# One token group of a mixer interleaved with the MLP before it, with the on-chip memory laid out from two sides

## The chip, the cores and the metric

The kernel runs on one core of one Trainium2 chip. The core has five engines that work side by side, each down its own list of instructions: PE (matrix multiplication), DVE (vector), ACT (scalar and activation functions), POOL (a second, general elementwise engine) and SP, which here only issues DMA transfers. They meet through semaphores. Data lies in device memory (HBM), in SBUF (the on-chip memory that all engines read) and in PSUM (eight banks of accumulators that PE writes). The metric is the device time of one execution in microseconds (us); lower is better. Before the change three runs took 2917.79, 2919.15 and 2923.32 us, median 2919.15 us.

## What is computed

One inference step of a two-layer hybrid decoder of width 1024, on 16 meta tokens and 1024 prompt tokens of one sequence and 8 decode tokens of other sequences, 1048 tokens in all, in float32. Cut to what matters:

```python
def _trunk(h, ...):
    for i in range(2):
        hn = _rmsnorm(h, norm_mix[i])
        if i == 0: out = _conformer_conv(hn, ...)   # gated projection, 31-tap causal conv, LayerNorm, SiLU, projection
        else:      out = _rwkv7(hn, ...)            # r, k, v projections, low-rank decay/gate, sequential state update
        h = h + out
        h = h + _sqrelu_mlp(_rmsnorm(h, norm_mlp[i]), w_mlp_in[i], w_mlp_out[i])
    return _rmsnorm(h, norm_final)

def _sqrelu_mlp(h, w_in, w_out):                    # 1024 -> 4096 -> 1024
    return jnp.square(jax.nn.relu(h @ w_in)) @ w_out

def _rwkv7(h, ...):
    prev = h shifted by one token;  xx = prev - h
    xr, xw, xk, xv, xa, xg = (h + xx * x_mix[j] for j in range(6))
    r, k, v = xr @ w_r, xk @ w_k, xv @ w_v
    decay, a, g = low-rank functions of xw, xa, xg
    ... a state update per token, a group norm, (yn + bonus) * g @ w_o
```

The new states (convolution rows, shifted row, the RWKV matrices) are outputs too.

## The kernel before

**Precision.** Every float32 product is three passes of PE (`mm3`, L185): weight and activation are each split into a high part (a cast on ACT, L157) and a low part, the difference (L162, on POOL in four pieces of 256 columns, or on DVE in one instruction of 1024), and PE computes high x high, low x high and high x low (L187 to L189).

**Weights.** `load_w` brings a 128 x 1024 block (512 KB) by a DMA on SP's list into a "raw" buffer (L146), and splits it into a "hi" and a "lo" buffer. A raw buffer comes free after the low part is made, hi and lo after the last matmul that reads them. The first layer has five raw and five split buffers for all its weights, the mixer three and four (`open_weights`), the rest five and five.

**Tokens.** The first layer works on three groups of 352, 348 and 348 tokens (`G0`), the mixer on four of 272, 256, 256 and 264 (`G1`), the end on three (`G2`). Between the layers the residual goes to HBM (`d_h`) and its normed form too (`d_hn`), and the mixer loads its own groups from `d_hn`.

**First layer.** For each group: `pw1` and the convolution (on DVE, in PSUM), `ln_silu`, then `post(g)`: the projection `pw2`, `mlp_in` (the norm's statistics and the split of the activations) and `mlp`. The MLP has 32 input blocks (`load_in`, `inp`, L327 to L329 and L141 behind the matmuls) and 32 output halves (`load_out`, `out`, L340), each block with 24 matmuls. Beside the MLP of one group run, as generators that `fill` advances at given points, the norm of the group before (`norm_out(g - 1)`, L591 to L605) and the convolution of the next. `norm_out(2)` stands behind the last MLP.

**Mixer.** Everything of the first layer is then closed (`with ExitStack() as l0`), its memory and PSUM handed to the mixer's pools: masks, `wk` (state of the recurrence), `tmp1`, `hnp`, weights, `mixp` (ten mixes), and the PSUM pools `psum1`, `psx1`, `psw`. `prepare(g)` loads the normed tokens and subtracts neighbours (L791). `mixer_in(g, tick, ahead)` makes eight mixes (L814, split by L140 and L141), eight r projections (copied by L965, stored to `d_rk` by L966), then the same for k with the gate's second layer, then for v with all that the recurrence needs (L1083 to L1126), stored to HBM. Beside the r projections runs the narrow first layer of the gate, beside the k projections that of decay and rate. Between the parts of each projection stands a call of `tick`, 72 in a group, which for groups 1 to 3 advances the recurrence over chunks of 64 tokens (`advance`) by a set pace; for group 0 the pace is 0, since no chunk is ready. In the front of each chunk L1214 masks a PSUM result into `nr`, once for each half.

**What sets the order.** The program is written in one order, with generators woven in by hand, and the tile framework's scheduler (`schedule_with_timeline_sim=True`) then places the instructions of every engine by that priority and its own estimate of times, subject to free buffers. On the chip each engine follows its list.

Of the kernel before, what the change touches and what calls it, by code (L numbers as in the profile page):

```python
# [16 lines left out]
P = 128  # L17
# [31 lines left out]
def hybrid_step(tc, x_prompt, x_sample, state_conv, state_shift, state_wkv, meta_tokens,  # L49
# [10 lines left out]
    with ctx:  # L60
# [63 lines left out]
        def open_tmp(stack, nmax, tag, bufs=3, **kw):  # L124
            cur["n"] = cur["wide"] = nmax
            cur["tmp"] = pool(stack, f"tmp{tag}", bufs, **kw)
            cur["stat"] = pool(stack, f"stat{tag}", 1, **kw)

        def stat(name, tag, bufs, w=None):
            return cur["stat"].tile([P, w or cur["n"]], F32, name=name, tag=tag, bufs=bufs)  # L130

        def open_weights(stack, raw_bufs, bufs, tag):
            if raw_bufs:
                cur["raw"] = pool(stack, f"wraw{tag}", raw_bufs)
            cur["wsp"] = pool(stack, f"wsp{tag}", 1)
            cur["bufs"] = bufs
# [12 lines left out]
        def load_w(src, shape, name, eng_lo, tag="w", raw=None):  # L149
# [4 lines left out]
            nb = cur["bufs"][tag]  # L154
            hi = cur["wsp"].tile([P, 8 * P], F32R, name=f"{name}_hi", tag=tag + "h", bufs=nb)
            lo = cur["wsp"].tile([P, 8 * P], F32R, name=f"{name}_lo", tag=tag + "l", bufs=nb)
# [16 lines left out]
        def col_stream(cols, raw_ahead, split_ahead, tag="w"):  # L173

            raws, parts = {}, {}
            for i in range(len(cols)):
                for j in range(i, min(i + raw_ahead + 1, len(cols))):
                    if j not in raws:
                        raws[j] = load_raw(col_src(*cols[j][:2]), (KT, P), cols[j][2])
                for j in range(i, min(i + split_ahead + 1, len(cols))):  # L180
                    if j not in parts:
                        parts[j] = load_w(None, (KT, P), cols[j][2], cols[j][3], tag, raws[j])
                yield parts[i]
# [7 lines left out]
        def bank(name, tag="mm"):  # L191
            return cur[tag].tile([P, 512], F32, name=name, tag=tag)

        def dense(w, act, n, name, fill=None):
            ps = bank(f"ps_{name}")
            for k in range(KT):
                mm3(ps[:, :n], (w[0][:, k, :], w[1][:, k, :]), (act[0][:, k, :n], act[1][:, k, :n]), k == 0, k == KT - 1)
                if fill and k == KT // 2 - 1:
                    fill()
            return ps  # L200
# [84 lines left out]
        def filler(points, *streams):  # L285
# [10 lines left out]
            return fill, chain.from_iterable(it for it, _ in its)  # L296
        MLP_POINTS = 6 * DFF // P
# [5 lines left out]
        def mlp(layer, groups, lag, eng_w, eng_h, fill=None, done=None):  # L303

# [14 lines left out]
            def inp(j, w, group):  # L319
# [4 lines left out]
                ps = dense(w, (ah, al), n, f"in{layer}_{j}_{gn}", fill)  # L324
# [7 lines left out]
            def out(b, i, w, group):  # L332
                gn, hv, n, ah, al, rs, hid_pool = group
                hh, hl = hid[gn, b]
                for m in range(4):
# [5 lines left out]
                    if fill:  # L341
                        fill()
# [1277 lines left out]
```

## Time and profile before

| | |
|---|---|
| median of three runs | 2919.15 us |
| the profiled execution, its span | 2917.4 us |
| mean granted clock of PE | 0.954 |
| DVE / ACT / POOL busy | 1974.6 / 1348.5 / 1698.8 us |
| DMA moved | 428.34 MB, mean 147 GB/s |
| projection pw2 of the last group | 822 to 863 us |
| MLP of the last group | 863 to 1122 us |
| from there to the first r projection of mixer group 0 | 1122 to 1149 us |
| mixer group 0, to the first r projection of group 1 | 1149 to 1302 us |

How to read it. The profile is one execution on the chip; the program's span there is 2917.4 us, and no other time is given for that execution. The page gives busy time by engine and the chain of work that ended last. A row of the view by stretches has start and end, length, the busy time of PE, of PE's weight loads, of DVE, ACT and POOL (with instruction counts), the granted clock of PE (1.00 is full), the busy share of the DMA engines and GB/s. In a timeline a row is start, duration, engine, line and operation, and in square brackets how long the engine had been idle and what ended that. A view of waits has who waited for whom: total us, times, longest. A group row has the operation, its tiles and shapes, the count, the busy time and the mean in ns, and the idle time before. Matmuls overlap, so their durations are longer than their distance from one another.

### The profile page before, as it was taken

The page shows a single profiled execution, that of the slowest core. Times are in us where ns is not written, and L with a number is a line of the kernel's source. Part 1 is how long each engine was busy: PE and PEld are TensorE (multiplying, and loading weights), DVE is VectorE, ACT ScalarE, POOL GpSimd, SP SyncE. Part 2 cuts the span into 40 slices and gives each one's busy share as a digit, 9 for nine tenths or more (in the row PEclk, how much of TensorE's full clock was granted, in tenths as well). Part 3 has the DMA queues.
Part 4 walks back from the last instruction along what each step waited for, and adds up shares of the span by engine and source line. Part 5 has one row for each costly group of instructions (what it writes and reads, how often), then busy time and mean ns, then how long its engine had stood idle before and what let it go on. Part 6 is the DMA issues. An engine that isn't in the chain of part 4 may idle for free.

```text
span 2917.4 us, 54478 instructions
## 1 busy us (share of the span) xinstructions
PE 2716.8 (93%) x20554; PEld 2578.6 (88%) x20554; DVE 1974.6 (68%) x3794; ACT 1348.5 (46%) x2515; POOL 1698.8 (58%) x2295
## 2 busy tenths in 40 slices
PE   8999999999999896879798899799999999999998
PEld 7988999999999896868688788677879999999998
DVE  5999999994554545477986885565697664444444
ACT  5546444543453333554667756443434453222223
POOL 6677778887797774443434454443447883333332
PEclk9999999999999998979899999889999999999999
DMA  6663444454444542667788867844557652222211
GB/s 176 172 183 95 149 139 134 140 173 138 138 139 142 173 130 89 203 190 193 195 201 228 229 189 185 228 108 124 139 134 218 184 158 84 70 68 68 71 59 40
DMA packets 659285, 428.34 MB, mean 147 GB/s; under 512 B 126840, under 2 KB 609208, under 8 KB 659022
## 3 DMA queue, kind: packets, MB, share of 16 engines
q1 hardware_dynamic: 652780, 421.93, 51.0%
q10 hardware_dynamic: 6018, 2.89, 0.4%
q8 instruction: 162, 2.65, 0.4%
q14 instruction: 101, 0.83, 0.1%
q0 software_dynamic: 224, 0.03, 0.0%
HBM read 353.03 MB, written 72.66 MB: 146 GB/s over the span
## 4 chain that ended last, share of the span: by engine, by line
PE 66%; DVE 13%; POOL 6%; DMA 5%; issue 4%; ACT 3%; SPq 0%; DVEq 0%; POOLq 0%; ACTq 0%
PE ps_in L189 7%; PE ps_in L187 7%; PE ps_in L188 7%; PE out L187 7%; PE out L189 7%; PE out L188 7%; POOL wo_lo L162 4%; POOL wi_lo L162 2%; DVE cv L504 2%; PE A L1206 2%; PE ps_o L189 1%; PE ps_o L188 1%; PE ps_o L187 1%; DVE mx L814 1%; PE ps_oo L187 1%
## 5 line engine op out<-in xcount | busy, mean ns | idle before, releaser
L162 POOL TENSOR_TENSOR wo_lo<-wo_raw,wo_hi 128x256 fp32r<-128x256 f32 x736 | 562.2, 796 | 300.0 <-ACT wo_hi L157 281.4
L162 POOL TENSOR_TENSOR wi_lo<-wi_raw,wi_hi 128x256 fp32r<-128x256 f32 x640 | 486.5, 792 | 308.2 <-ACT wi_hi L157 292.3
L187 PE MATMUL out<-hh,wo_hi 128*128 128x352 f32 (+2 forms) x1536 | 503.5, 328 | 21.0 <-DVE h L340 10.4
L340 DVE TENSOR_TENSOR h<-h,out 128x352 f32<-128x352 f32 (+2 forms) x768 | 385.3, 510 | 199.3 <-PE out L189 198.8
L189 PE MATMUL out<-hl,wo_hi 128*128 128x352 f32 (+2 forms) x1536 | 494.5, 324 | 7.0 <-DVE hl L141 7.0
L187 PE MATMUL ps_in<-m_h,wi_hi 128*128 128x352 f32 (+2 forms) x1536 | 498.4, 325 | 0.7 <-DVE h L340 0.7
L189 PE MATMUL ps_in<-m_l,wi_hi 128*128 128x352 f32 (+2 forms) x1536 | 498.2, 325 | 0.0
L188 PE MATMUL out<-hh,wo_lo 128*128 128x352 f32 (+2 forms) x1536 | 497.7, 324 | 0.0
L188 PE MATMUL ps_in<-m_h,wi_lo 128*128 128x352 f32 (+2 forms) x1536 | 497.0, 324 | 0.0
L504 DVE SCALAR_TENSOR_TENSOR cv<-u,wdw,cv 128x352 f32<-128x352 f32 (+2 forms) x720 | 376.9, 573 | 0.7
L157 ACT CAST wi_hi<-wi_raw 128x1024 fp32r<-128x1024 f32 x160 | 167.7, 1048 | 401.6 <-PE out L189 205.3
L157 ACT CAST wo_hi<-wo_raw 128x1024 fp32r<-128x1024 f32 x184 | 192.9, 1049 | 302.8 <-PE out L189 144.8
L187 PEld LDWEIGHTS out<-hh,wo_hi 128*128 128x128 f32 x1536 | 291.8, 190 | 28.1 <-DVE h L340 14.0
L189 PEld LDWEIGHTS out<-hl,wo_hi 128*128 128x128 f32 x1536 | 291.2, 190 | 9.4 <-DVE hl L141 8.3
L187 PEld LDWEIGHTS ps_in<-m_h,wi_hi 128*128 128x128 f32 x1536 | 291.2, 190 | 3.0 <-issue 0.9
L188 PEld LDWEIGHTS out<-hh,wo_lo 128*128 128x128 f32 x1536 | 291.8, 190 | 1.4
L189 PEld LDWEIGHTS ps_in<-m_l,wi_hi 128*128 128x128 f32 x1536 | 291.0, 190 | 2.0
L188 PEld LDWEIGHTS ps_in<-m_h,wi_lo 128*128 128x128 f32 x1536 | 290.9, 189 | 1.7
L327 DVE SCALAR_TENSOR_TENSOR r<-ps_in,rs_m 128x352 f32<-128x352 f32 (+2 forms) x192 | 98.6, 515 | 228.2 <-PE ps_in L189 224.5
L141 DVE TENSOR_TENSOR hl<-s,hh 128x352 fp32r<-128x352 f32 (+2 forms) x192 | 150.2, 783 | 102.4 <-ACT hh L140 102.3
L329 ACT ACTIVATE s<-r 128x352 f32<-128x352 f32 (+2 forms) x192 | 93.8, 490 | 146.8 <-DVE r L327 146.4
L162 POOL TENSOR_TENSOR wv_lo<-wv_raw,wv_hi 128x256 fp32r<-128x256 f32 x96 | 80.3, 866 | 28.9 <-ACT wv_hi L157 28.8
(407 smaller groups left out, 6248.1 us busy)
## 6 DMA issues: line engine op xcount, KB each, us to landing
wi_raw<-in_w_mlp_in_dram SPq DMA_DIRECT2D x160, 512.0 KB
wo_raw<-in_w_mlp_out_dram SPq DMA_DIRECT2D x160, 512.0 KB
wr_raw<-in_rwkv_w_r_dram SPq DMA_DIRECT2D x32, 512.0 KB
wk_raw<-in_rwkv_w_k_dram SPq DMA_DIRECT2D x32, 512.0 KB
wv_raw<-in_rwkv_w_v_dram SPq DMA_DIRECT2D x32, 512.0 KB
d_ab<-ab SPq DMA_DIRECT2D x32, 512.0 KB
pg_raw<-in_conv_w_pw_dram SPq DMA_DIRECT2D x24, 512.0 KB
pa_raw<-in_conv_w_pw_dram SPq DMA_DIRECT2D x24, 512.0 KB
```

The lines of the kernel that those rows point to most:

```text
L141: eng_lo.tensor_sub(lo, src, hi.bitcast(F32))
L157: nc.scalar.copy(hi[:, :a * b], raw[:, :a * b])
L162: eng_lo.tensor_sub(lo[:, cs], raw[:, cs], hi[:, cs].bitcast(F32))
L187: nc.tensor.matmul(ps, w[0], act[0], start=first, stop=False)
L188: nc.tensor.matmul(ps, w[1], act[0], start=False, stop=False)
L189: nc.tensor.matmul(ps, w[0], act[1], start=False, stop=last)
L327: nc.vector.scalar_tensor_tensor(r[:, :n], ps[:, :n], 0.0, rs[:, :n], op0=ALU.max, op1=ALU.mult)
L329: nc.scalar.activation(s[:, :n], r[:, :n], AF.Square)
L340: nc.vector.tensor_add(hv[:, 4 * i + m, :], hv[:, 4 * i + m, :], ps[:, :n])
L504: nc.vector.scalar_tensor_tensor(acc[m][:, :n], ug[:, m, j:j + n], wdw[:, m, j:j + 1], acc[m][:, :n], op0=ALU.mult, op1=ALU.add)
L814: nc.vector.scalar_tensor_tensor(t[:, :n], xx[:, k, :n], vec("x_mix", i * KT + k), hx[:, k, 1:1 + n], op0=ALU.mult, op1=ALU.add)
L1206: nc.tensor.matmul(ps[:, i * 2 * P:(i + 1) * 2 * P], bk[:, j + i, :], xa[:, j + i].rearrange("p q x -> p (q x)"), start=True, stop=True)
```

## The change

1. **The last group's MLP becomes a generator** that the mixer's first group advances. `mlp` is split into `mlp_steps` (191 steps) and a loop; `dense` into `dense_steps` and a loop. `post(2)` ends before its MLP. `mlp2` is the chain of that MLP and of `norm_out(2)`; eight steps are taken at once (`HEAD`), one at each of the nine steps of `prepare(0)`, and 2.6 (`STEPS`) at each tick of group 0. What is left is run before group 1.
2. **`norm_out(1)`** is filled into the last `pw2` and no longer into the last MLP.
3. **Memory from two sides.** What the last MLP needs lies on the right (its activations, residual, hidden tiles, temporaries, statistics); what only the earlier part needs lies on the left in a stack of its own (`le`), closed before the mixer, whose pools then open on the left. `wk`, `tmp1`, the mixer's PSUM pools and the state of the recurrence open only before group 1.
4. **Rings of weight blocks.** A `Ring` takes buffers in turn from several pools. Pool a has 2 raw and 3 split blocks, pool b 2 and 2; the first part also has 1 raw block more (e). While the MLP and group 0 run together the mixer uses a alone and the MLP b alone. From group 1 on the mixer has a and c (2 + 1 raw, 3 + 1 split), the last layer a and f (2 + 3, 3 + 2). The blocks of the second low-rank layers (`second`) always take their split buffers from a. Mixes: nine for group 0, then ten. PSUM: five matmul banks and two more while both run, one for statistics; from group 1 on four, one and three as before.
5. **The low parts of the last MLP's blocks** whose names end in 1, 4 or 7 are made by DVE, the rest by POOL as before.
6. `nr` is written by one instruction for both halves; in `col_stream` a block is split before later blocks are loaded.

The diff, cut to its core:

```diff
+        class Ring:
+            def __init__(self, *parts):
+                self.order = [(pl, n) for pl, n in parts for _ in range(n)]
+                self.i = 0
+            def tile(self, shape, dtype, name, tag):
+                pl, n = self.order[self.i % len(self.order)]
+                self.i += 1
+                return pl.tile(shape, dtype, name=name, tag=tag, bufs=n)
...
+        HEAD = 8
+        STEPS = 2.6
...
         def mlp(layer, groups, lag, eng_w, eng_h, fill=None, done=None):
+            for _ in mlp_steps(layer, groups, lag, eng_w, eng_h, done):
+                if fill:
+                    fill()
...
+        right = dict(side="right")
+        raw_a, wsp_a = raw_pool(ra, "a", 2, **right), split_pool(ra, "a", 3, **right)
...
+            raw_b, wsp_b = raw_pool(l0, "b", 2, **right), split_pool(l0, "b", 2, **right)
+            open_tmp(l0, N0, "0", **right)
+            resid_r = pool(l0, "resid01", 1, **right)
+            act_r = pool(l0, "actp01", 1, **right)
+            upool = pool(le, "upool", 1)
...
-                pw2(g, ln_act[g], add)
+                early = [(([ranked(CV, norm_out(1))], KT + 1 + MW))] if g == 2 else []
+                fill, rest = filler(2 * KT, *early)
+                pw2(g, ln_act[g], add, fill)
...
+                if g == 2:
+                    return group
...
-            for g in range(3):
+            for g in range(2):
                 post(g)
-            for _ in norm_out(2):
-                pass
+            group = post(2)
+
+        ring_a = rings((raw_a,), (wsp_a,))
+        ring_b = rings((raw_b,), (wsp_b,))
+        cur.update(ring_a)
+        cur["mm"] = Ring((psum0, 5), (pool(ps0, "psum0b", 2, space=PSUM), 2))
+        MW0 = lambda name: nc.vector if name.endswith(MLP_DVE) else nc.gpsimd
+        MLP_DVE = ("1", "4", "7")
+        mlp2 = chain(mlp_steps(0, [group], 2, MW0, nc.vector), norm_out(2))
+
+        def beside_mixer(steps):
+            cur.update(ring_b)
+            for _ in range(steps):
+                next(mlp2, None)
+            cur.update(ring_a)
+        beside_mixer(HEAD)
...
-                    nc.vector.tensor_mul(nr[:, j:j + 2, q, :], pv[:, :, q, HS:], mk[:, :, HS:])
+                nc.vector.tensor_mul(nr[:, j:j + 2], pv[..., HS:], mk[:, :, HS:].unsqueeze(1).broadcast_to([P, 2, 2, HS]))
...
         def tick(g, slow):
+            if g == 0:
+                cur["due"] += STEPS
+                beside_mixer(int(cur["due"]))
+                cur["due"] %= 1
+                return
             advance(PACE[g] * slow, NCH - 1)
             next(ng0, None)
...
         for g in range(4):
             if g == 0:
                 for _ in prepare(0):
+                    beside_mixer(1)
+            if g == 1:
+                cur.update(ring_b)
+                for _ in mlp2:
                     pass
+                l0.close()
+                ps0.close()
+                cur["wk"] = pool(lw, "wk", 1, **right)
+                open_tmp(ld, N1, "1", 3, **right)
+                raw_c, wsp_c = raw_pool(ld, "c", 1, **right), split_pool(ld, "c", 1, **right)
+                cur.update(rings((raw_a, raw_c), (wsp_a, wsp_c)))
...
+                cur["mm"] = pool(lm, "psum1", 4, space=PSUM)
+                cur["x"] = pool(lm, "psx1", 1, space=PSUM)
+                cur["w"] = pool(lm, "psw", 3, space=PSUM)
+                open_recurrence()
             mixer_in(g, lambda slow=1.0: tick(g, slow), ranked(PP, prepare(g + 1)) if g < 3 else iter(()))
```

More of the change, by code (lines that the diff above doesn't have):

```diff
@@ L197, in dense @@
                 mm3(ps[:, :n], (w[0][:, k, :], w[1][:, k, :]), (act[0][:, k, :n], act[1][:, k, :n]), k == 0, k == KT - 1)
-                if fill and k == KT // 2 - 1:
+                if k == KT // 2 - 1:
+                    yield
+            return ps
+        def dense(w, act, n, name, fill=None):
+            it = dense_steps(w, act, n, name)
+            while True:
+                try:
+                    next(it)
+                except StopIteration as e:
+                    return e.value
+                if fill:
                     fill()
-            return ps
         def new_act(pl, name, nmax, tag="act"):
@@ L323, in inp @@
                 hh, hl = hid[gn, j // 2]
-                ps = dense(w, (ah, al), n, f"in{layer}_{j}_{gn}", fill)
+                ps = yield from dense_steps(w, (ah, al), n, f"in{layer}_{j}_{gn}")
                 with tc.high_priority(offset=HR):
@@ L346, in outs @@
                     for group in groups:
-                        out(b, i, w, group)
+                        yield from out(b, i, w, group)
             last = nj - 1
@@ L362, in mlp @@
             for group in groups:
-                inp(last, w, group)
+                yield from inp(last, w, group)
                 for i in range(2):
-                    out(nj // 2 - 1, i, wo[i], group)
+                    yield from out(nj // 2 - 1, i, wo[i], group)
                 if done and group is not groups[-1]:
                     done(group[0])
-        with ExitStack() as l0:
-            cur["mm"] = pool(l0, "psum0", 5, space=PSUM)
-            cur["x"] = pool(l0, "psx0", 1, space=PSUM)
-            psc = pool(l0, "psc", 2, space=PSUM)
-            upool = pool(l0, "upool", 1)
-            actp = [pool(l0, f"actp0{i}", 1) for i in range(2)]
-            residp = [pool(l0, "resid00", 1)]
-            cur["raw"] = pool(l0, "wraw0", 5)
-            open_tmp(l0, N0, "0")
-            residp.append(pool(l0, "resid01", 1))
-            open_weights(l0, 0, {"w": 5}, 0)
+        right = dict(side="right")
@@ L576, in ln_silu, with pw2 @@
                     yield 1
-            def pw2(g, act, add):
+            def pw2(g, act, add, fill):
                 n = G0[g][1]
@@ L626, in post @@
                 fill, rest = filler(MLP_POINTS, *streams)
[L627 removed]
+                mlp(0, [group], 2, nc.gpsimd, nc.vector, fill)
                 for _ in rest:
```

129 lines of the change are left out of this document (78 added, 51 removed).

## The prediction

> **What bounds the kernel now.** I read the page first, then the share of work by stretches, then the timeline of the stretch that the change touches.
>
> ```profile
> span 2917.4 us, 54478 instructions
> PE 2716.8 (93%) x20554; PEld 2578.6 (88%) x20554; DVE 1974.6 (68%) x3794; ACT 1348.5 (46%) x2515; POOL 1698.8 (58%) x2295
> PE 66%; DVE 13%; POOL 6%; DMA 5%; issue 4%; ACT 3%; SPq 0%; DVEq 0%; POOLq 0%; ACTq 0%
> ```
>
> PE (the matrix engine) is busy for 93% and holds 66% of the chain that ended last: only time in which PE idles or runs at a reduced clock can be won. The span is 2917.4 us, the median of the three runs 2919.15 us; I sum against the span and add 1.75 us.
>
> The stretches (length, busy time by engine, granted clock, DMA share, GB/s): the last pw2, the start of the last group's MLP, that MLP, the pause behind it, the first mixer group, and the last four together.
>
> ```profile
> 822.00:863.00 41.00, 38.75 (x243) 38.24 (x242) 20.82 (x30) 25.16 (x44) 37.31 (x46) 1.00 0.46 131
> 863.00:873.00 10.00, 10.00 (x59) 9.18 (x58) 4.54 (x4) 4.18 (x7) 10.00 (x16) 1.00 0.59 187
> 873.00:1122.00 249.00, 237.88 (x1471) 235.59 (x1470) 127.49 (x224) 93.93 (x130) 177.64 (x246) 0.98 0.46 139
> 1122.00:1149.00 27.00, 4.71 (x8) 2.52 (x8) 10.97 (x14) 5.33 (x15) 13.15 (x23) 0.57 0.32 112
> 1149.00:1302.00 153.00, 126.19 (x1063) 118.75 (x1063) 91.94 (x152) 87.90 (x203) 63.39 (x88) 0.86 0.65 186
> 863.00:1302.00 439.00, 378.77 (x2599) 366.04 (x2597) 234.94 (x391) 191.33 (x353) 264.19 (x371) 0.91 0.52 155
> ```
>
> In 439 us PE idles for 60.2 us (439 - 378.8). Three places show how, and what follows a wait (start, duration, what, in brackets the idle time before it and what ended it):
>
> ```profile
> 1128.06 2.69 PE L231 MATMUL st_d<-acc_d,ones_d 128*128 128x348 f32 x4 [6.59 <-POOL acc_d L253]
> 1149.25 0.59 PE L187 MATMUL p_r<-mh,wr_hi 128*128 128x272 f32 x1 [16.48 <-ACT mh L140]
> 1287.87 0.60 PE L187 MATMUL p_v<-mh,wv_hi 128*128 128x272 f32 x1 [4.49 <-ACT wa L1083]
> 1288.26 0.43 PE L188 MATMUL p_v<-mh,wv_lo 128*128 128x272 f32 x1
> 1292.79 0.29 PE L187 MATMUL p_v<-mh,wv_hi 128*128 128x272 f32 x1
> ```
>
> The waits of PE in the mixer group (total, times, longest):
>
> ```profile
> PE p_v L187 <- ACT wa L1083: 4.7, 2, 4.5
> PE pb L740 <- DVE rk L1094: 4.2, 2, 3.4
> PE p_k L189 <- POOL ml L141: 4.1, 1, 4.1
> PE l_a L187 <- ACT wa L1083: 3.8, 1, 3.8
> ```
>
> The group norm behind the MLP, the reload of its result and the first mixes hold PE from 1122 to 1149; inside the mixer short waits for ACT and DVE recur. After the 4.49 us wait the matmuls stay at 0.43 us until 1292.79, where they are 0.29: almost 5 us of slow clock behind one pause.
>
> **The work that must be done.** A full-speed MLP shows the pitch, and the chain of waits the sums of the norm ahead of it:
>
> ```profile
> 900.00:950.00 50.00, 50.00 (x318) 50.00 (x317) 21.12 (x39) 18.91 (x25) 39.06 (x54) 1.00 0.46 141
> 863.67 2.34 PE st_m L231 x8
> ```
>
> 50 / 318 = 0.157 us a matmul. The MLP of a group has 64 weight blocks with 24 matmuls each, 1536: 241.2 us. The mixer group is 126.2 x 0.86 = 108.5 us at full clock, the pause 4.7 x 0.57 = 2.7, the norm's sums 2.3. Together 355 us against 439: **84 us is the most that can be won here**, 60 of it idle and 24 reduced clock.
>
> By the Trainium skill (TensorE: Matmul & The Clock Gate, section on the HAM clock gate) PE falls to half clock after about 3.4 us of idling and needs about 3.4 us of work to return. The trace agrees in kind, with almost 5 us where the page has 3.4. By the page's figure the six waits of 3.4 us and more in the rows above would lose 6 x 1.7 = 10 us instead of 24, and the most to be won would be 70 instead of 84.
>
> **Part 1: interleaving.** The MLP as a generator has 2 x 31 + 1 + 16 x 8 = 191 steps (1.26 us of PE each), the norm behind it 17. 8 run ahead, 9 in the mixer's preparation, 2.6 at each of the 72 ticks of group 0: the MLP's end falls at tick (191 - 17) / 2.6 = 67. Every mixer wait of up to 2.6 x 1.26 = 3.3 us a tick gets PE work in front of it, and the pause of 27 us disappears, because group 0 reads only tokens 0 to 271, whose norm was stored long before.
>
> What can fill PE is limited by the weights. The MLP's blocks now have two raw and two split buffers of their own, where five and five were shared. One block costs:
>
> ```profile
> L162 POOL TENSOR_TENSOR wo_lo<-wo_raw,wo_hi 128x256 fp32r<-128x256 f32 x128 | 96.4, 785 | 21.8 <-ACT wo_hi L157 21.8
> L157 ACT CAST wo_hi<-wo_raw 128x1024 fp32r<-128x1024 f32 x31 | 32.5, 1049 | 53.5 <-PE ps_in L189 26.1 <-PE out L189 25.8 <-POOL wi_lo L162 1.6
> L162 DVE TENSOR_TENSOR wr_lo<-wr_raw,wr_hi 128x1024 fp32r<-128x1024 f32 x3 | 3.5, 1218 | 0.0
> 1175.53 0.52 SPq L938 DMA_DIRECT2D wg_raw<-in_rwkv_g_dram  x1
> 1181.01 1.05 ACT L157 CAST wg_hi<-wg_raw 128x1024 fp32r<-128x1024 f32 x1 [3.21 <-DMA wg_raw<-in_rwkv_g_dram]
> ```
>
> A 512 KB load took 5.5 us from issue to the cast that waited for it; the cast 1.05; the subtraction 4 x 0.785 = 3.1 on POOL or 1.22 on DVE. Names ending in 1, 4, 7 go to DVE: 10 of the 32 input blocks and 16 of the 32 output halves (all with i = 1), 26 of 64. Mean subtraction (38 x 3.1 + 26 x 1.22) / 64 = 2.3. A raw buffer is held for 8.9 us plus queueing q; two buffers give one block in (8.9 + q) / 2, 64 blocks in 285 us at q = 0. That is below 355, so the ring bounds only when q exceeds 2.2 us a block, and it eats the whole gain at 64 (8.9 + q) / 2 = 433, q = 4.6 (6 us kept for the end). A split buffer is held 1.05 + 2.3 + 5.5 (355 / 64): also 8.9.
>
> Queues passed: all these loads stand on SP's one list, so the 64 MLP loads now stand between the mixer's stores, which wait for compute. SP's longest waits for stores before (r of the mixer; the MLP's normed result):
>
> ```profile
> SPq L966 <- ACT st L965: 27.2, 6, 15.9
> SPq L605 <- DVE h L602: 19.4, 1, 19.4
> ```
>
> The r stores wait 4.5 us each, in six places only; behind them stand the next MLP loads. DVE gets 26 x 1.22 = 32 us more, minus some 10 of group 1's norm that leaves: 257 us; POOL falls to 264 - 26 x 3.1 = 183. Neither is full. The mixer's own ring falls to two raw and three split blocks for group 0; with one block held by the second-layer weights and one by the narrow ones, the k weights are single-buffered, 1.05 + 1.22 = 2.3 us each, hidden behind the 3.3 us of MLP at the tick ahead (nine mixes instead of ten likewise); without that cover 8 x 2.3 = 18 us.
>
> How well PE is filled, from stretches in which other work runs beside:
>
> ```profile
> 286.00:550.00 264.00, 256.89 (x1584) 253.09 (x1584) 257.57 (x514) 122.45 (x192) 212.04 (x288) 0.99 0.47 142
> 1302.00:1850.00 548.00, 486.73 (x5538) 439.37 (x5539) 436.09 (x892) 348.52 (x814) 254.10 (x353) 0.93 0.76 199
> ```
>
> MLP beside convolution: 256.9 x 0.99 / 264 = 96%. Mixer beside recurrence: 486.7 x 0.93 / 548 = 83%. The new stretch is two thirds MLP by PE time but with shallow rings: I take 91%, 355 / 0.91 = 390 us (ends 370 and 428).
>
> The end: memory and PSUM of the MLP must come free before group 1, the recurrence and their buffers, whose ten memsets stood on POOL ahead of the norm's last addition and now stand at the change to group 1:
>
> ```profile
> 1121.74 0.46 POOL sv L1147
> 1126.60 0.52 POOL xa L1188
> 1127.12 0.89 POOL acc_d L253
> ```
>
> The norm's store, for which SP waited 19.4 us, can hold group 1's loads. Bounds 0 (the MLP ends five ticks early, its norm runs beside) and 24 us (the pause before, less its work); I take 6, nearer to the first, as group 1's tokens don't need that norm. Gain 439 - 390 - 6 = **43 us**; ends 69 and -13.
>
> **Part 2: group 1's norm moves from that MLP into the last pw2.** Before, it and the mixer's preparation stopped the MLP's epilogue on DVE:
>
> ```profile
> 970.51 6.70 DVE L602 SCALAR_TENSOR_TENSOR h<-h,pvec,rs_d 128x348 f32<-128x348 f32 x8
> 977.13 5.35 DVE L791 TENSOR_TENSOR xx<-hx 128x272 f32<-128x272 f32 x6
> ```
>
> That idle time is in the 60 us already. In pw2 DVE has room (20.8 of 41), POOL hardly (37.3 of 41), and five additions of 0.89 (the acc_d row above) come to it; the norm's two stores join SP's list there. Bounds 0 and 6 us lost (the additions and one more behind them), taken 3.
>
> **Part 3: nr in one instruction for two halves**, 17 x 4 pairs.
>
> ```profile
> L1214 DVE TENSOR_TENSOR nr<-A,m_ar x136: 269/275/294, 1332.9 to 2165.8; 128x128 f32<-128x128 f32 x136
> L1063 DVE TENSOR_TENSOR bv<-vv,pk x32: 403/414/440, 1254.0 to 1867.7; 128x256 f32<-128x256 f32 x16, 128x272 f32<-128x272 f32 x8, 128x264 f32<-128x264 f32 x8
> ```
>
> The nearest row of 256 columns out of PSUM takes 0.41: 68 x (0.55 - 0.41) = 9.5 us of DVE, in a stretch with DVE at 80% (436 of 548). Bounds 0 and 9.5, taken 3 for the chain's DVE share and its neighbours. From group 1 on the rings again add up to three raw, four split and ten mixes; in the last layer five and five; in the first part five and five: nothing.
>
> **Sum:** 2917.4 - 43 + 3 - 3 = 2874.4, with 1.75: **2876 us**.
>
> **The rivals.** *Starved ring (slower).* The MLP's two-deep ring takes the bound. It decides from q = 4.6 us a block. If each block meets one store wait of 4.5 us on SP and one DVE subtraction of 1.2 in front of its own, q = 5.7: 64 x 14.6 / 2 = 467 us, with the end 473, 34 slower: 2953 us. For it: an engine works off the list that the planner wrote, so a late MLP block also holds the mixer's matmuls listed behind it. Also this, DVE at the start of the MLP:
>
> ```profile
> 869.10 0.95 DVE L327 SCALAR_TENSOR_TENSOR r<-ps_in,rs_m 128x348 f32<-128x348 f32 x2
> 871.74 7.47 DVE L141 TENSOR_TENSOR hl<-s,hh 128x348 fp32r<-128x348 f32 x2 [1.69 <-ACT hh L140]
> ```
>
> Two operations of a size for which L327 needs 0.95 took 7.5 while POOL was full (10.0 of 10): DVE and POOL do hold each other up. The Trainium skill says so (SBUF — State Buffer, section on the two separate sides): a DVE operation with two SBUF inputs and a GpSimd operation that reads SBUF exclude each other for a whole instruction. By that rule the 26 moved subtractions block POOL for 32 us, 0.5 a block. Against the rival: POOL falls to 183 of some 390 us, and six store waits are not 64. Chance 0.13.
>
> *Near the floor.* The mixer has no weight trouble and PE is at 96%: 370 + 2, gain 67: 2852 us. For it the convolution's stretch, with DVE at 98%. Chance 0.19.
>
> *No interleaving in effect.* The planner orders each engine by its own estimate; where it runs the MLP first, only the norm's 6.7 us of DVE leave it, and cost as much in pw2; nr's 3 us remain: 2916. Against: it already places the mixer's xx at 977 in the MLP. Chance 0.06.
>
> **How the numbers follow.** Forecast 0.62, near the floor 0.19, no interleaving 0.06, starved 0.13. 0.2% is 5.8 us, about what a measurement can tell. Faster 0.81 (forecast and floor), same 0.06, slower 0.13. The range: below, the floor case with all 9.5 of part 3, 2846; above, the forecast with the 83% stretch (428 + 6, gain 5: 2914) and pw2's other 3, 2917, which also holds the third rival. The forecast's own range, with 94 and 88% in place of 91, is 2864 to 2889.
>
> **What would show it.** Right: out and ps_in matmuls of group 2 between p_r, p_k and p_v of group 0; PE above 90% and clock above 0.95 there; no pause of over 10 us before group 1; group 1's first p_r about 40 us earlier; nr x68 near 0.41. Wrong: PE waiting for wi_lo, wo_lo or their casts (ring), SP waiting for POOL or DVE on MLP loads while PE idles, a pause at the change to group 1, or pw2 growing by over 6 us.

## The result and the profile after

| | before | after |
|---|---|---|
| median (lowest to highest, runs) | 2920.75 us (2917.79 to 2923.32, 4) | 2870.16 us (2869.81 to 2873.75, 4) |
| span of the profiled execution | 2917.4 us | 2872.0 us |
| mean granted clock of PE | 0.954 | 0.957 |

The ratio is 0.9831, with a 95% interval of 0.9815 to 0.9846: 50.6 us less by the medians, 45.4 us by the two profiled spans (the profiled execution of the kernel after is the slowest of its four). The page of the kernel after, its head, its share of busy time and the chain that ended last:

```profile
span 2872.0 us, 54182 instructions
PE 2708.4 (94%) x20554; PEld 2579.9 (90%) x20554; DVE 1986.7 (69%) x3752; ACT 1348.8 (47%) x2517; POOL 1627.1 (57%) x2191
PE 21%; POOL 1%; DVE 1%; issue 1%; DMA 1%; ACT 0%; SPq 0%; DVEq 0%; ACTq 0%; POOLq 0%
```

PE has the same 20554 matmuls and is busy for 2708.4 us instead of 2716.8: of the 45.4 us some 8 are matmuls that run at a better clock or overlap more, and 37 are idle time that is gone. The chain is cut off early here (its shares add up to 25%), so I don't read it.

The time at which certain work starts (the first matmul of each kind in PE's timeline, us from the span's start) shows where the gain was made:

| | before | after | difference |
|---|---|---|---|
| first MLP matmul of the last group | 859.2 | 861.9 | +2.7 |
| first r projection of mixer group 0 | 1149.3 | 897.5 | |
| last MLP matmul of the last group ends | 1121.5 | 1234.9 | |
| last v projection of group 0 ends | 1298.9 | 1245.8 | -53.1 |
| first r projection of group 1 | 1302.3 | 1247.3 | -55.0 |
| first k projection of group 1 | 1344.4 | 1302.3 | -42.0 |
| first r projection of group 3 | 1677.4 | 1655.1 | -22.3 |
| first k projection of group 3 | 1719.9 | 1707.8 | -12.1 |
| first `ps_oo` of the last layer | 1874.8 | 1876.6 | +1.8 |
| last layer's MLP, first input block | 1962.7 | 1923.9 | -38.8 |
| `ps_oo` of the last layer's second group | 2336.3 | 2288.9 | -47.4 |
| the end | 2917.4 | 2872.0 | -45.4 |

The whole gain is there when group 1 begins, 13 us of it are lost in group 1's r projections, and from then on the lead swings between nothing and 47 us.

By stretches, the kernel after (length, busy time of PE, weight loads, DVE, ACT and POOL, granted clock, DMA share, GB/s): the last pw2, the MLP alone, the MLP beside the mixer, the end of that, all three of these together, and group 1's r projections.

```profile
822.00:862.00 40.00, 37.73 (x220) 36.51 (x219) 23.74 (x34) 21.49 (x36) 27.85 (x35) 0.96 0.42 125
862.00:900.00 38.00, 29.59 (x153) 26.85 (x154) 31.76 (x54) 19.43 (x40) 29.64 (x44) 0.87 0.60 168
900.00:1140.00 240.00, 236.71 (x1574) 234.87 (x1573) 120.74 (x185) 103.34 (x162) 109.88 (x138) 0.99 0.52 155
1140.00:1247.00 107.00, 102.16 (x890) 97.94 (x888) 89.75 (x159) 66.82 (x151) 58.18 (x80) 0.97 0.72 208
862.00:1247.00 385.00, 368.46 (x2612) 359.67 (x2612) 242.24 (x396) 189.58 (x352) 197.70 (x261) 0.97 0.58 171
1247.00:1302.00 55.00, 42.05 (x298) 38.40 (x297) 43.31 (x93) 23.89 (x56) 27.62 (x41) 0.78 0.78 203
```

What was one average before falls into three different parts. In the middle PE is filled to 236.71 x 0.99 / 240 = 97.6%, more than I had taken even for the favourable rival. In the first 38 us it is 29.59 x 0.87 / 38 = 68%, a loss of 12 us; in the last 107 us 93%, a loss of 8.

The waits of PE between 862 and 1247 are short now (who waited for whom, total, times, longest), and SP still waits:

```profile
PE out L211 <- ACT wo_hi L177: 4.5, 2, 3.6
PE out L211 <- DVE r L369: 2.6, 1, 2.6
PE pk L1124 <- DVE h L382: 2.1, 1, 2.1
PE out L212 <- DVE wo_lo L182: 1.9, 1, 1.9
...
SPq L165 <- POOL wi_lo L182: 48.7, 19, 4.5
SPq L165 <- POOL wo_lo L182: 38.6, 13, 6.2
...
SPq L1029 <- ACT st L1028: 21.7, 8, 5.5
```

PE idles for 16.5 us (385 - 368.46) where it idled for 60. SP waits for raw buffers and for the r stores as forecast, but little of that reaches PE. Half of PE's 16.5 us, 8.4, lie in the first 38 us.

### The profile page after: what moved, and what is told of

The parts are those of the page before. It is cut to its first block, busy times and chain, and to the rows that moved or that the text cites. A ratio compares the mean times of both kernels' runs of the same rounds, so it can differ in the third digit from the quotient of the medians.

```text
span 2872.0 us, 54182 instructions
## 1 busy us (share of the span) xinstructions
PE 2708.4 (94%) x20554; PEld 2579.9 (90%) x20554; DVE 1986.7 (69%) x3752; ACT 1348.8 (47%) x2517; POOL 1627.1 (57%) x2191
## 5 line engine op out<-in xcount | busy, mean ns | idle before, releaser
L182 POOL TENSOR_TENSOR wo_lo<-wo_raw,wo_hi 128x256 fp32r<-128x256 f32 x672 | 517.1, 801 | 333.9 <-ACT wo_hi L177 287.5
L182 POOL TENSOR_TENSOR wi_lo<-wi_raw,wi_hi 128x256 fp32r<-128x256 f32 x600 | 462.7, 802 | 331.2 <-ACT wi_hi L177 318.3
L211 PEld LDWEIGHTS out<-hh,wo_hi 128*128 128x128 f32 x1536 | 292.8, 191 | 27.3 <-DVE h L382 11.2
L160 DVE TENSOR_TENSOR hl<-s,hh 128x352 fp32r<-128x352 f32 (+2 forms) x192 | 138.3, 721 | 97.7 <-ACT hh L159 97.4
```

The lines of the kernel that those rows point to most:

```text
L160: eng_lo.tensor_sub(lo, src, hi.bitcast(F32))
L182: eng_lo.tensor_sub(lo[:, cs], raw[:, cs], hi[:, cs].bitcast(F32))
L211: nc.tensor.matmul(ps, w[0], act[0], start=first, stop=False)
```

## The experiments

### Is it the order written by hand, and not the memory or the rings?

All of the MLP is put ahead of the mixer, everything else stays:

```diff
-        HEAD = 8
+        HEAD = 1000
```

> The changed kernel with all 208 steps of the last MLP and its norm taken ahead of the mixer (HEAD 1000 in place of 8); memory, rings, the DVE share of the low parts and the norm's place in pw2 stay as in the changed kernel (2870.2 us). Theory (the weaving by hand is what fills PE): the MLP stands alone again on its two-deep rings, (8.9 + q) / 2 = 4.5 us a block against 3.8 of PE, 64 blocks 285 us, then the mixer group of about 153 us less what starts early: 2905 to 2935 us, near the kernel before. Rival (the two sides of memory alone bring the gain, because the mixer's buffers no longer wait for the MLP's end and the scheduler can place mixer work into its gaps by itself): 2870 to 2885 us, with p_r matmuls between those of the MLP.

Measured: 2915.73 us (2906.89 to 2921.23, 10 runs) against 2921.53 for the kernel before beside it, ratio 0.9974 (0.9960 to 0.9988). Its stretches: the MLP's start, its rest, and from there to group 1's first r projection at 1308.6.

```profile
859.00:900.00 41.00, 34.91 (x186) 31.61 (x185) 27.32 (x50) 19.35 (x37) 28.05 (x45) 0.92 0.61 177
900.00:1132.00 232.00, 222.16 (x1360) 215.06 (x1359) 121.68 (x203) 85.60 (x121) 104.05 (x136) 1.00 0.43 127
1132.00:1308.00 176.00, 134.48 (x1052) 122.90 (x1054) 102.67 (x158) 86.17 (x196) 67.71 (x94) 0.84 0.61 173
```

The pause of 27 us behind the MLP is gone here too (the r projections begin at 1132.2, the MLP ends at 1132.4), but the MLP takes 273 us (859.2 to 1132.4) instead of 262 (859.2 to 1121.5), and the mixer alone leaves PE at clock 0.84 with 42 us idle in 176. What the change wins it wins by having MLP matmuls listed between the mixer's: the planner doesn't do that by itself. The longer MLP also shows the price of its own rings when it runs alone: PE waits there for casts and low parts of its blocks, 14.0 us in all, and in the kernel before, with five buffers, for none.

### Do the two raw buffers bound the MLP?

One of the MLP's two raw buffers is kept out of use while both run:

```diff
-            raw_b, wsp_b = raw_pool(l0, "b", 2, **right), split_pool(...)
+            raw_b, raw_b2, wsp_b = raw_pool(l0, "b", 1, **right), raw_pool(l0, "b2", 1, **right), split_pool(...)
```

(The first part still uses all; `ring_b` holds only `raw_b`.)

> The changed kernel with one raw buffer for the MLP while it runs beside mixer group 0 (two before; the second still serves the first part). It measures how long one block holds a raw buffer: 64 blocks one after the other. Theory (8.9 us worked out from load, cast and low part, with little queueing): 64 x 8.9 = 570 us for the stretch of 385, so about 3055 us, and PE waits for the MLP's casts; the hold that is measured, halved, says how far the two-deep ring was from binding (it binds at 5.5 us a block, 11.1 us of hold). Rival (the ring was close to binding, hold 11 us or more): 64 x 11 = 704 us, 3190 us or more. If the stretch grows by less than 100 us, both are wrong and a load takes much less than 5.5 us.

Measured: 3033.52 us (2 runs), ratio 1.0371 (1.0338 to 1.0403). The stretch of the MLP and the mixer, then what PE waits for in it, and ACT in its turn:

```profile
862.00:1383.00 521.00, 411.30 (x2558) 385.51 (x2557) 235.86 (x391) 187.64 (x344) 185.18 (x258) 0.91 0.42 122
```

```profile
PE out L211 <- ACT wo_hi L177: 54.0, 25, 4.3
PE ps_in L211 <- ACT wi_hi L177: 32.5, 20, 3.5
...
ACT wi_hi L177 <- DMA wi_raw<-in_w_mlp_in_dram: 96.7, 22, 7.8
ACT wo_hi L177 <- DMA wo_raw<-in_w_mlp_out_dram: 95.0, 25, 6.9
```

Now the ring is the bound, and it can be seen as that: PE waits for the casts of the MLP's blocks, and the casts for their loads. The MLP's 64 blocks take 518 us (859.0 to 1377.2), 8.1 us each: that is the time for which one raw buffer is held, with the queueing behind stores in it. With two buffers a block can come every 4.05 us, and in the changed kernel one is needed every 373 / 64 = 5.8 us. So over the stretch as a whole the raw ring didn't bind. In the changed kernel the casts wait rather for PE to give a split buffer back, which is to say that the weights are there before PE needs them (view of waits, 862 to 1247):

```profile
ACT wo_hi L177 <- PE ps_in L213: 48.2, 16, 5.8
ACT wi_hi L177 <- PE out L213: 41.6, 17, 5.0
```

The two split buffers were not varied by a run.

### The subtractions on DVE

All low parts of the last MLP go back to POOL:

```diff
-        MLP_DVE = ("1", "4", "7")
+        MLP_DVE = ("none",)
```

> The changed kernel with all 64 low parts of the last MLP on POOL (26 of them on DVE before). POOL gets 26 x 3.1 = 81 us more (198 to 279 of 385 us), DVE 32 us less. Theory (PE is the bound inside the stretch, a block takes (9.7 + q) / 2 on the ring, 5.5 on PE): 0 to 8 us slower, 2870 to 2878 us. Rival (the relief of POOL decides, its list being the MLP's and the mixer's at once): 20 to 40 us slower, 2890 to 2910 us. Third: DVE is the tighter engine towards the end of the stretch, then it is faster by 2 to 5 us.

Measured: 2866.47 us (2865.76 to 2873.16, 4 runs), ratio 0.9805 (0.9786 to 0.9824). From the MLP's start to group 1's first r projection it takes 389.1 us instead of 385.4. The choice of engine is worth some 4 us at that place, and nothing that can be told from the scatter in the whole.

### More steps a tick

```diff
-        STEPS = 2.6
+        STEPS = 3.0
```

> The changed kernel with 3.0 steps of the MLP at a tick in place of 2.6: the MLP ends at tick 58 of 72 in place of 67, its norm at tick 64. Theory (the r projections of group 1 take 54.5 us in the changed kernel against 41.5 before because the last group's norm, the memsets and the opening of the recurrence's memory fall on them): they shrink to 42 to 48 us, the v projections without cover cost 2 to 8 us, sum 2858 to 2870 us. Rival (those 13 us hang on the opening of the buffers at the change to group 1 itself, wherever the MLP ends): they stay at 52 to 57 us and the run takes 2870 to 2880 us.

Measured: 2874.57 us (2867.6 to 2877.92), ratio 0.9830 (0.9810 to 0.9851): no gain. Group 1's r projections are even shorter than hoped, 31 us (1276.1 to 1307.1) instead of 54.5, but group 0's last projection still ends at 1246.3, and between the two stands a new wait. PE's timeline at that point:

```profile
1245.99 0.29 PE L213 MATMUL p_v<-ml,wv_hi 128*128 128x272 f32 x1
...
1246.96 0.73 PE L1124 MATMUL pk<-rk,hsum 128*128 128x272 f32 x2
1271.24 5.43 PE L1273 MATMUL A<-xa,bk 128*128 128x256 f32 x12 [23.55 <-DMA bk<-d_ab]
1276.13 0.65 PE L211 MATMUL p_r<-mh,wr_hi 128*128 128x256 f32 x1
```

The planner put the recurrence's first products ahead of group 1's projections in PE's list, and they wait 23.55 us for `bk`, which comes from group 0 by way of HBM (`d_ab`). Group 1's k projections begin at 1307.6, later than the 1302.3 of the changed kernel. A step that ends earlier bought nothing, because the order changed behind it. In these 24 us the mixes could run ahead of PE, so the 31 us don't show by themselves what the norm and the memsets cost group 1.

### nr in one instruction, undone alone

```diff
-                nc.vector.tensor_mul(nr[:, j:j + 2], pv[..., HS:], mk[:, :, HS:].unsqueeze(1).broadcast_to([P, 2, 2, HS]))
+                    nc.vector.tensor_mul(nr[:, j:j + 2, q, :], pv[:, :, q, HS:], mk[:, :, HS:])
```

> The changed kernel with nr written by two instructions as before. 68 x 0.14 = 9.5 us more on DVE between 1280 and 2120 us. Theory of the prediction: 3 us slower (0 to 9.5), 2870 to 2880 us, likeliest 2873. Rival (the recurrence or PE sets the pace there, DVE's time is free): within 1 us, the recurrence from its first to its last A product still 836 us.

Measured: 2847.47 us (2844.4 to 2852.99), ratio 0.9740 (0.9717 to 0.9762): 22.7 us faster than the change. The instruction itself does what was forecast of it (count, then min/median/max in ns; the kernel after, then this one):

```profile
L1281 DVE TENSOR_TENSOR nr<-A,m_ar x68: 402/405/425, 1288.8 to 2121.4; 128x256 f32<-128x256 f32 x68
```

```profile
L1281 DVE TENSOR_TENSOR nr<-A,m_ar x136: 269/282/293, 1287.8 to 2088.9; 128x128 f32<-128x128 f32 x136
```

68 x 0.405 = 27.5 us of DVE against 136 x 0.282 = 38.4. Less work on DVE, and a later end. The same edit was then made alone in the kernel before (one instruction in place of two there):

> The kernel before with one edit of the change alone, nr in one instruction. The changed kernel became 23 us faster when nr went back to two instructions (2870.2 to 2847.5), and big matmuls were followed by small ones of the recurrence 159 times there in PE's list, 112 times with two instructions. Theory A (the single instruction is itself slower for the recurrence, which waits for both halves): the kernel before becomes 10 to 25 us slower, 2930 to 2945 us. Theory B (nr only shifts the scheduler's list, and the alternations carry the time; here they go from 227 to 224): within 5 us of the kernel before, 2914 to 2925 us.

Measured: 2936.43 us (2930.66 to 2942.36, 6 runs) against 2924.35, ratio 1.0043 (1.0027 to 1.0059): 12 us slower. With two pairs it looked like a real cost of the merged instruction.

### Is it large and small matmuls in turn on PE?

Where the lists of the first kernels differed, one thing stood out: how often PE changes from a full-width matmul to one of the recurrence's small ones, 159 times in the changed kernel, 112 with nr in two instructions. The timeline of the kernel after shows what such a stretch looks like, with no idle time in it:

```profile
1954.10 0.41 PE L211 MATMUL out<-hh,wo_hi 128*128 128x328 f32 x1
1954.44 0.33 PE L1374 MATMUL Y<-uv,nr 128*64 128x64 f32 x2
1954.70 0.42 PE L212 MATMUL out<-hh,wo_lo 128*128 128x328 f32 x1
...
1962.28 0.64 PE L213 MATMUL out<-hl,wo_hi 128*128 128x328 f32 x1
1962.85 0.31 PE L1309 MATMUL gg<-x,no 32*32 32x32 f32 x2
1963.09 0.64 PE L211 MATMUL out<-hh,wo_hi 128*128 128x328 f32 x1
```

So the recurrence's small matmuls were put first in the planner's order, in one block each, and nothing else changed (the same around the matmuls of gg, W, U, S and Y):

```diff
-            for p in range(KT):
-                for q in range(2):
-                    nc.tensor.matmul(ps[HALF[q], ...
+            with tc.high_priority(offset=1000):
+                for p in range(KT):
+                    for q in range(2):
+                        nc.tensor.matmul(ps[HALF[q], ...
```

> The changed kernel with the small matmuls of the recurrence (gg, po, W, U, S, Y) put ahead of other work in the scheduler's priority, so that they stand together in PE's list: big matmuls are followed by a small one of the recurrence 77 times in place of 159. Theory B (each alternation of a big and a 32- or 64-wide matmul costs 0.35 to 0.7 us: 0.57 us in the timeline where a big one at full clock takes 0.16, and its pair on the way back): 82 x 0.35 to 0.7 = 29 to 57 us faster, 2813 to 2841 us. Rival A (nr's single instruction is what costs): 2865 to 2875 us. Rival C (the time after group 0 is set by the recurrence's own chain, DVE and ACT between its products): up to 10 us either way, the recurrence from first to last A product still 836 us.

Measured: 2864.74 us (2863.18 to 2868.74), ratio 0.9800 (0.9785 to 0.9815), though the changes fall from 159 to 77. The same in the kernel before:

> The kernel before with the same priority for the recurrence's small matmuls and nothing else: 103 alternations in place of 227. Theory B: 124 x 0.35 to 0.7 = 43 to 87 us faster, 2834 to 2878 us, all of it behind group 0. Then what the change itself won is to be read at the first r projection of group 1, and this gain is one apart from it. Rival C: within 10 us of 2921 us.

Measured: 2918.1 us (2904.6 to 2920.48, 10 runs), ratio 0.9975 (0.9962 to 0.9988), with 227 changes down to 103. Halving the changes is worth 5 us and 6 us by the medians, not the tens that this theory needed; as an account of the total it falls. By stretches a gain is there and is lost again elsewhere:

| | last layer's first input block to the second group's `ps_oo` | from group 1's first k projection to that block |
|---|---|---|
| the change | 365.0 to 338.8 | 621.6 to 641.3 |
| the change, nr in two (run below) | 343.8 to 341.3 | 615.8 to 635.6 |
| the kernel before | 373.6 to 357.9 | 618.4 to 626.7 |

Each entry is without and with the priority. In all three pairs the last layer becomes shorter and what stands ahead of it longer. That the others lose there by standing behind the small ones is an argument, not shown.

### Does merged nr cost, or is it the planner's order that falls differently?

Four more kernels with nr in two instructions: one where both stand behind the copies and masks, at the place of the merged one, and the partners of three kernels above.

```diff
-                nc.vector.tensor_mul(nr[:, j:j + 2], pv[..., HS:], mk[:, :, HS:].unsqueeze(1).broadcast_to([P, 2, 2, HS]))
+                for q in range(2):
+                    nc.vector.tensor_mul(nr[:, j:j + 2, q, :], pv[:, :, q, HS:], mk[:, :, HS:])
```

> The changed kernel with nr written by two instructions of 128 columns again, but both behind the copies and the other masks of the pair, where the merged one stands; nothing else differs. If the merged instruction itself is what costs (its 0.405 us against twice 0.275), this gives back what the two-instruction version gave: 2844 to 2856 us. If only the place in the order counted, it stays at 2866 to 2876. If neither is a cause and each edit merely throws the planner's order anew, any time from 2845 to 2890 is possible, and a third value, outside both bands, is what would show it.

Measured: 2856.99 us (2851.75 to 2859.83), ratio 0.9782 (0.9764 to 0.9799), 1 us outside the first band and far from the second. So the place in the order is not what cost, as far as one draw can say; yet the same two instructions at another place differ by 9.5 us (2847.47 against 2856.99).

> The version in which the recurrence's small matmuls stand first (2864.7 us with merged nr), with nr in two instructions. If merged nr costs 12 to 25 us whatever stands around it: 2840 to 2853. If the difference seen so far was the planner's placement, its sign is open here: 2853 to 2885 would speak for that, most plainly above 2865.

Measured: 2862.69 us (2858.02 to 2869.22), ratio 0.9805 (0.9786 to 0.9824).

> The version whose low parts are all made on POOL (2866.5 us with merged nr), with nr in two instructions. If merged nr costs 12 to 25 us whatever stands around it: 2841 to 2855. If it is placement: a difference under 8 us or of the other sign, 2858 to 2890.

Measured: 2863.97 us (2861.89 to 2866.91), ratio 0.9808 (0.9794 to 0.9823).

> The version with 3.0 steps a tick (2874.6 us with merged nr), with nr in two instructions. If merged nr costs 12 to 25 us whatever stands around it: 2850 to 2863. If it is placement: a difference under 8 us or of the other sign, 2866 to 2895.

Measured: 2885.75 us (2880.11 to 2887.53), ratio 0.9876 (0.9858 to 0.9893). The wait of 24.7 us in front of the first A product is here as well.

| the pair's surroundings | nr merged | nr in two | merged minus two |
|---|---|---|---|
| the change | 2870.16 | 2847.47 | +22.7 |
| the kernel before | 2936.43 | 2924.35 | +12.1 |
| small matmuls first | 2864.74 | 2862.69 | +2.1 |
| all low parts on POOL | 2866.47 | 2863.97 | +2.5 |
| 3.0 steps a tick | 2874.57 | 2885.75 | -11.2 |

The sign changes; the two small differences lie inside the runs' scatter, and by the ratios to the kernel before beside them both have the other sign. The mean of the five is +5.6 us, and with their spread (standard deviation 12.6) its standard error is 5.7: no systematic cost is shown, nor the gain of 3 that I had forecast. What is shown is that an edit of this size moves the end by anything from -11 to +23 us. The rest of the program says the same. From group 1's first k projection to the end the following kernels have the same text as the changed one, and the same work:

| | first k projection of group 1 | from there to the end | matmuls in the last layer's stretch | its length |
|---|---|---|---|---|
| the change | 1302.3 | 1569.7 | 2914 | 365.0 |
| all low parts on POOL | 1303.4 | 1560.7 | 2872 | 354.4 |
| 3.0 steps a tick | 1307.6 | 1562.9 | 2888 | 357.3 |
| MLP ahead of the mixer | 1361.4 | 1543.8 | 2858 | 352.3 |
| one raw buffer | 1438.4 | 1598.3 | 2914 | 364.8 |
| (nr in two, otherwise the change) | 1299.8 | 1544.0 | 2816 | 343.8 |
| (the kernel before) | 1344.4 | 1573.0 | 3038 | 373.6 |

The last layer's stretch runs from its first input block to the second group's `ps_oo`; the matmuls are counted in PE's list between these two, and what varies in their number are those of the recurrence that are left over.

Equal text takes 1543.8 to 1598.3 us in these traces. A part of that is scatter: the runs of one kernel lie within 4 to 16 us of each other, the profiled execution with the MLP ahead is the fastest of ten (2906.89, median 2915.73), and the one with one raw buffer the slower of two (3038.53, median 3033.52). If the whole distance to the median lies in this part, equal text takes 1553 to 1593 us, and 1553 to 1566 without the kernel with one raw buffer. The rest is fixed in the program, as the counts show: in its lists the planner places instructions otherwise when something ahead of them has changed. The length of the last layer's stretch follows the count. In the nine kernels that are the change but for one or two edits, the priority aside, it is 343.8 us with 2816 matmuls, 352.3 with 2858, 354.4 with 2872, 357.2 and 357.3 with 2888, and 362.3 to 365.9 with 2914. The part ahead of it shows no such rule. Where the difference sits can be read by stretches, the changed kernel and the one with nr in two (the mixer's groups 1 to 3 with the recurrence, then the last layer's first MLP beside the recurrence's end):

```profile
1302.00:1846.00 544.00, 480.96 (x5378) 428.53 (x5377) 405.44 (x787) 338.05 (x787) 236.60 (x340) 0.91 0.75 195
...
1924.00:2289.00 365.00, 352.54 (x2915) 314.54 (x2916) 256.15 (x504) 162.20 (x305) 224.21 (x276) 0.94 0.59 163
```

```profile
1300.00:1836.00 536.00, 473.08 (x5403) 420.49 (x5401) 406.74 (x829) 339.65 (x792) 241.31 (x347) 0.92 0.75 197
...
1915.00:2259.00 344.00, 328.15 (x2814) 298.20 (x2815) 254.67 (x512) 156.73 (x294) 216.49 (x270) 0.97 0.59 165
```

By the starts of the groups' matmuls 21.2 of the 28.2 us between the two spans lie in the last layer's stretch (365.0 against 343.8 us), at a lower clock (0.94 against 0.97) and with 98 matmuls more by PE's list, left over from the recurrence. Which single decision of the planner sends them there is not settled.

## Why the prediction was right, step by step

**Part 1, the interleaving: right, and by the mechanism named.** From the first MLP matmul to group 1's first r projection it was 443.1 us before (859.2 to 1302.3) and is 385.4 (861.9 to 1247.3); 390 was forecast for it from 863 on, where the stretch was 439, so the gain is 57.7 us and not 49. The other kernels that weave the same way with 2.6 steps take 383.3 to 389.1, and the three traces in the kernel before's order 439.8 to 443.1. Filled against the 355 us floor that is 92%, where 91% was taken. The average is right and its make-up isn't: beside the mixer PE is at 97.6%, as the rival near the floor had it, and the loss sits where the MLP still runs alone ahead of the first mixes (12 us) and at the end (8 us). The kernel with the MLP ahead of the mixer (2915.73) shows that memory and rings don't bring this without the hand-woven order; it is also what the rival without interleaving would have given, 2916.

**The ring: right beside the mixer, not where the MLP runs alone.** It was to bound only when the queueing reached 2.2 us a block. The kernel with one raw buffer measured 8.1 us a block, held and queued, against 8.9 without any queueing: that sum was too large, and a two-deep ring delivers in 4.05 us what is needed every 5.8. SP's waits (87.3 us behind POOL's low parts, 21.7 us behind the r stores) are in the trace, yet cost PE next to nothing beside the mixer. Alone, the MLP at the prediction's 0.157 us a matmul uses up a block in 3.8 us, faster than 4.05, and there the sign that was named for the ring does appear: of PE's 8.4 idle us in the first 38, 8.3 are waits for casts and low parts of the MLP's blocks. The longest, and ACT ahead of it:

```profile
885.61 0.49 ACT L371 ACTIVATE s<-r 128x348 f32<-128x348 f32 x1 [2.59 <-DVE r L369]
886.52 1.04 ACT L177 CAST wo_hi<-wo_raw 128x1024 fp32r<-128x1024 f32 x1
887.61 1.24 PE L211 MATMUL out<-hh,wo_hi 128*128 128x348 f32 x3 [3.64 <-ACT wo_hi L177]
```

That cast stands on ACT behind a step that waits for DVE, so the order of ACT's list has a share in it; it is not separated from the ring's. The 26 subtractions on DVE made no difference that can be told from the planner's scatter (2866.47 us with all of them on POOL). By the Trainium skill (SBUF — State Buffer, section on the two separate sides) DVE and POOL would exclude each other there for whole instructions; the two DVE operations at 871.74 us that the prediction shows agree in kind, but no run here puts a price on it.

**The end: the place right, the size off.** 6 us were taken, with a bound of 24; it is 13.0 (group 1's r projections take 54.5 us instead of 41.5). The longest wait of these projections and that of the recurrence's first product between them, and what DVE and POOL did (timeline of the kernel after):

```profile
1249.27 2.52 DVE L651 SCALAR_TENSOR_TENSOR h<-h,pvec,rs_d 128x348 f32<-128x348 f32 x4
1252.13 2.11 DVE L651 SCALAR_TENSOR_TENSOR h<-h,pvec,rs_d 128x348 f32<-128x348 f32 x4
1260.84 0.58 PE L213 MATMUL p_r<-ml,wr_hi 128*128 128x256 f32 x1 [3.68 <-DVE ml L160]
1262.35 2.19 POOL L1217 MEMSET xa<- 64x512 f32 x4 [0.71 <-DMA d_hn<-h]
1264.57 2.19 POOL L1255 MEMSET xa<- 64x512 f32 x4
1289.35 2.04 PE L1273 MATMUL A<-xa,bk 128*128 128x256 f32 x4 [3.92 <-DVE nr L1281]
```

The norm of the last group (`h` by `pvec`, 4.6 us of DVE) falls between group 1's mixes, and the recurrence's memsets come on POOL behind that norm's store and ahead of the next low part of a mix, as forecast. I had taken the small value because group 1's tokens don't need that norm; they don't, but their mixes share its engines. From the stretches, 9 us of the 13 are idle PE (12.95 against 4.0) and 4 are clock (0.78 against 0.88); the same stretch before:

```profile
1302.00:1344.00 42.00, 38.00 (x294) 36.45 (x295) 33.65 (x73) 18.06 (x45) 19.57 (x22) 0.88 0.75 194
```

Of the 12.95 us, 3.92 are the wait for `nr`, which neither the norm nor the memsets explain. How much of the rest is theirs stays open, since no run moves them alone.

**Part 2, the norm moved into the last pw2: right.** 3 us taken, 2.7 by the start of the MLP. That start by itself moves between 856.3 and 862.4 us from trace to trace, so the better measure is the distance from the end of the MLP before: 30.3 us in the three traces with the norm in its old place, 32.5 to 33.1 in the eleven with it in pw2.

**Part 3, nr: the step that failed**, though it hardly shows in the sum. "Bounds 0 and 9.5, taken 3" supposed that a saving on DVE can only help and that everything else stays in its place. DVE did save 10.9 us; the end moved by +22.7, +12.1, +2.1, +2.5 and -11.2 us in five surroundings. Whatever is edited in a program that is planned as a whole, the term for its order has bounds on both sides, here -11 and +23 us in five surroundings, and I had none.

**The clock behind a wait: read too simply.** The prediction put almost 5 us of slow clock down to the pause of 4.49 us before 1287.87. It did not start with that pause: in the kernel before, the matmul at 1282.72 already takes 0.43 us, where the same kind takes 0.29 before 1282.4.

```profile
1282.72 0.43 PE L188 MATMUL l_a<-lah,wa_lo 128*128 128x272 f32 x1
```

So this row does not show by itself that the pause lowers the clock. The sum doesn't rest on it; its 24 us of reduced clock come from the stretches.

**The sum.** To group 1's k projections: forecast -49 + 6 + 3 = -40, measured -57.7 + 13.0 + 2.7 = -42.0. The agreement to 2 us is better than its terms: the interleaving won 8.7 us more than forecast and the end cost 7 more, and the two offset each other. The rest: forecast -3, measured -3.3 (1573.0 to 1569.7). That agreement is luck: by the medians the whole gain is 50.6 us, which would leave about -9 for it, and the same text, 1566 us in the change when moved to its median, took 1553 to 1593 elsewhere. Only the first is a success of the working. The version with nr in two instructions, 2847.47 us, is the fastest of all measured. Its last layer's stretch has the fewest matmuls left over from the recurrence; what in the edit made the planner order it so I cannot name.

## What to carry to other kernels

When independent dense work with no waits of its own can be woven between steps that wait, price it as the floor of PE's work in that stretch divided by a fill read from like stretches of the same kernel (here 92% came out), and put the doubt at its two ends, where only one of the two runs, not in the middle (here 97.6%). Check a shallow ring by its hold time per block, and by a run with one buffer less, which measures that time directly. And where a planner orders the engines, a small edit can move the end by 10 to 20 us either way: take the effect of a change from the stretch in which it acts, and call a change of the total a cause only after the same edit in several surroundings keeps its sign.

## What the runs showed of the hardware that was not expected

PE can be slow without a single idle entry. In the rows at 1954 us above, a matmul of 328 columns followed by two of 64 takes 0.60 us for the three (1954.10 to 1954.70), while the clock is full: the first of the small ones starts only 0.34 us behind the large one. Over the last layer's stretch of this trace, at full clock and without idle time between, a large MLP matmul is followed by a small one of the recurrence after 0.344 us (median of 78) and by another large one after 0.150 us (median of 1317), a difference of 0.19 us a change. By the Trainium skill (TensorE: Matmul & The Clock Gate, section on what happens when a matmul is issued) the drain of one matmul overlaps the next, and a single bf16 matmul takes (398 + N) / 2.4 ns, which for 328 columns makes an estimated 0.30 us. The 0.34 us lie near the second, as if between unlike matmuls this overlap were missing; no run tests that.

By stretches, this and what follows in the kernel after:

```profile
1950.00:1955.00 5.00, 5.00 (x35) 3.24 (x34) 2.74 (x5) 3.13 (x5) 3.75 (x5) 1.00 0.51 105
1955.00:1960.00 5.00, 5.00 (x28) 3.17 (x27) 0.50 (x1) 1.82 (x3) 1.87 (x2) 1.00 0.36 114
1960.00:1965.00 5.00, 5.00 (x22) 2.96 (x21) 0.50 (x1) 0.00 (x0) 0.00 (x0) 0.61 0.64 138
1965.00:1970.00 5.00, 5.00 (x28) 4.47 (x28) 0.99 (x2) 2.31 (x4) 2.79 (x4) 0.50 0.00 0
```

PE is busy for 5.00 of 5.00 us throughout, yet some 17 us after large and small matmuls begin to alternate (1943.67) the granted clock falls: 0.61 is the mean of a stretch that begins at full clock, 0.50 what is left, and the large matmul goes from 0.41 to 0.64 us. A busy PE is thus no proof of a full clock; whether the alternation lowers it was not tried by itself, and the two runs that halved the changes won only 5 and 6 us.
